# A gated short-convolution layer on one core: SyncE and VectorE held to the plan's order in the first stage, high part's products first

## The chip, the core and the metric

The kernel runs on one core of one Trainium2 chip. The metric is the device time of one execution in microseconds (us). Five engines work side by side: TensorE (PE in the profile, with its weight loads as PEld), VectorE (DVE), ScalarE (ACT), GpSimd (POOL) and SyncE (SP), which here does nothing but issue DMA transfers. Each engine takes its instructions strictly in the order in which they stand on it, and waits at an instruction whose semaphores are not yet there; what stands behind waits too.

## The reference

One layer of a decoder trunk (T = 256 tokens, D = 2048, E = 4096), all in float32:

```
h    = rmsnorm(x, norm_g)                                # (256, 2048)
mod  = silu(c) @ ada_w + ada_b                           # (6144): shift, scale, gate
h    = h * (1 + scale) + shift
b, cg, v, g = split(h @ sc_w_in, 4)                      # four parts of (256, 4096)
u    = causal_conv(cg * v, sc_conv_w)                    # width 3, each channel by itself
y    = (b * u * silu(g)) @ sc_w_out                      # (256, 2048)
out  = rmsnorm(x + gate * y, final_g)
```

## The kernel before

**Precision.** Every float32 product is made of three products of a reduced float32 form (fp32r). A weight is split into a high part (a cast on ScalarE, `split_hi`, L356) and a low part (weight minus high part on VectorE, `split_lo`, L361); the tokens are split the same way (`hh_` and `hl_`, both in the tile hT). A product is high x high, high x low tokens, low x high tokens: three matmuls, all from line L496.

**Stages.** The first stage (up to about 378 us) makes the first 16 of the 32 column tiles of all four parts; the second stage (tile mm_b) makes the other 16; the third multiplies with w_out and ends the layer. The change is in the first stage alone.

**Why the first stage is cut into passes.** The tokens can be multiplied only when shift and scale are known, and for these 32 MB of ada_w have to be read. So the 16 blocks of 128 token features (k = 0 to 15) become ready two at a time. A group of two blocks takes eight *adaLN pieces*: each is two transfers of 256 KB on SyncE (L464, tile at, four buffers) and two weighted sums on VectorE (L476 and L478, tile gv). After the eighth, `ada_done` transposes the sums on TensorE (L486, tp_g), adds them up on VectorE (L487, gs), adds the biases (L326, mod), and makes the block's high part on ScalarE (L330) and its low part on VectorE (L334 scales, L337 subtracts).

A *pass* (`part`) is for one chunk of 512 columns (ch) of one of the four parts (q), over the blocks k0 to k1 that are ready; there are 16 pairs of ch and q. The weights come from w_in by SyncE in slots (L540, tile raw_s): a full slot holds four blocks of 128 x 512 (1 MB), a half slot two (512 KB). A block costs 12 matmuls (`chunk_products`: four column tiles m, three products each). The pass's result in PSUM (mm_s) is kept: the first pass of a pair is copied by ScalarE (L518, tile acc, named by ch and q: acc20 is chunk 2, part 0). A later pass either starts with that sum in PSUM (a *seed*, a copy by ScalarE, L530, before the pass, and L518 behind it) or is added by VectorE (L520).

**What sets the order.** `plan()` walks through the stage with costs from constants (LOAD and ALOAD for transfers, PRODUCTS for a block's matmuls, and so on) and returns a list of steps, passes and adaLN pieces mixed: the earlier tokens are ready, the more blocks the later passes take. The code is written out in this order. But the scheduler of the tile framework then orders each engine's instructions by its own estimates; pieces have a lower priority (`later(GIVE)`), the end of a group a higher one (`later(-LEAD)`). Only the part before the first pass is fixed (`in_order`), and a few casts and low parts are held behind named instructions (`behind`): the casts of passes 2 to 9 behind the copy of the pass three before them, the low parts of passes 4 and 5 behind an adaLN sum.

In this document pass n is the n-th pass in the plan. Up to pass 19 the passes have the same blocks in both plans. Passes 1 to 13 take blocks 0 and 1 (24 matmuls each), 14 to 16 take blocks 0 to 3 (48), 17 to 19 blocks 2 and 3 (24).

The order of matmuls in a pass before: for each block, each m, the three products in turn, so that the low part is needed by the third matmul. Passes 2 and 3 alone do all products of the high part first.

Of the kernel before, what the change touches and what calls it, by code (L numbers as in the profile page):

```python
# [17 lines left out]
KT = D // P  # L18
# [15 lines left out]

LOAD = 0.19
ALOAD = 1.55
PRODUCTS = 0.343
VBLOCK = 0.143  # L40
VPIECE = 1.5
# [1 line left out]
SBLOCK = 0.119  # L43
SCOPY = 1.03
SSEED = 2.05
WLAG = 6.0
ALAG = 9.0
WAHEAD = 14.0
AAHEAD = 6.0
# [2 lines left out]
def plan():  # L52
# [4 lines left out]
    steps, ready = [], [0.0] * ADA[0]  # L57
    done = {}
    pieces = [(sum(ADA[:g]), nk, i) for g, nk in enumerate(ADA) if g for i in range(4 * nk)]
    load, pe, dve, act = 0.0, 4.0, 0.0, 0.0  # L60
    burst = SLOT // P

    def ada():
# [54 lines left out]
def short_conv_layer(ctx: ExitStack, tc: tile.TileContext, x, c, norm_g, ada_w, ada_b, w_in, conv_w, w_out, final_g, out):  # L118
    nc = tc.nc
# [43 lines left out]
    after = mybir.DependencyInfo(mybir.DependencyClass.NoSync, mybir.DependencyReason.DATA)  # L163

    @contextmanager
    def in_order():

        traced = nc.cur_bb.bb.instructions
        n = len(traced)
        yield  # L170
        last = {}
        for ins in list(traced[n:]):
            if ins.engine in last:
                tc.add_manual_dep(ins, last[ins.engine], after, reason="in order")
            last[ins.engine] = ins.name
        ended.update(last)

    @contextmanager
    def behind(last):
# [17 lines left out]
        col = QUARTERS[0] * E  # L197
        nc.sync.dma_start(raw[:, k * CT * P : (k + 1) * CT * P], w_in[0, k * P : (k + 1) * P, col : col + CT * P])

    ended = {}  # L200
    pinned = ctx.enter_context(ExitStack())
    pinned.enter_context(in_order())

# [247 lines left out]
    acc = {}  # L451
    sums = {}

    def ada_piece(k0, nk, piece):
        w = nk * P
        kk = ASLOT // (2 * w)
        if piece == 0:
            sums[k0] = adap.tile([P, 2, 2 * P], F32, tag="gv", name="gv")
        gv = sums[k0][:, :, 0:w]
        j = piece * kk  # L460
        at = adap.tile([P, ASLOT], F32, tag="at", name="at", bufs=4)
        at4 = at.rearrange("p (k s f) -> p k s f", k=kk, s=2)
        for s in range(2):
            nc.sync.dma_start(at4[:, :, s, :], adas[:, j : j + kk, s, k0 * P : k0 * P + w])  # L464
        with later(GIVE):
            ada_sums(j, kk, at4, gv)
        if j + kk == KT:
            with later(-LEAD):
                ada_done(k0, nk, gv)

    def ada_sums(j, kk, at4, gv):
        for i in range(kk):
            c_k = silu_c[:, j + i : j + i + 1]
            if j + i == 0:
                with behind(ended):
                    nc.vector.tensor_scalar_mul(gv, at4[:, i], c_k)  # L476
            else:
                nc.vector.scalar_tensor_tensor(out=gv, in0=at4[:, i], scalar=c_k, in1=gv, op0=ALU.mult, op1=ALU.add)  # L478
        added.append({ins.engine: ins.name for ins in nc.cur_bb.bb.instructions[-1:]})

    def ada_done(k0, nk, gv):

# [29 lines left out]
    kept, added = [], []  # L512

    def keep(ch, q, k0, bank, seed=False):
        if k0 == 0 or seed:
# [6 lines left out]
    def part(ch, q, k0, k1, seed):  # L522
# [13 lines left out]
        for s0 in range(k0, k1, step):  # L536
            sk = min(step, k1 - s0)
            n = sk * CT * P
            raw, hi, lo = places(n)
            nc.sync.dma_start(  # L540
                raw[:, :n].rearrange("p (k f) -> p k f", k=sk),
                w_in[0, s0 * P : (s0 + sk) * P, col : col + CT * P].rearrange("(k p) f -> p k f", p=P),
            )
            at = len(acc) if k0 == 0 else KT
            with behind(ended if at < 3 else kept[at - 3] if at < 9 else {}):
                split_hi(raw, n, hi)
            with behind(ended if at < 3 else added[at - 3] if at < 5 else {}):
                split_lo(raw, n, hi, lo=lo)
            for parts in ((0, 1), (2,)) if 0 < len(acc) < 3 else ((0, 1, 2),):
                for i in range(sk):  # L550
                    chunk_products(bank, hi, lo, i * CT * P, s0 + i, k0, k1, seed, parts=parts)
        if len(acc) == 1:
# [18 lines left out]
            split_y(ys[-1], vq)  # L571

    LATER = (10, 14)
    whole = [0] * NCH
    for kind, *step in plan():
        if kind == "ada":
            ada_piece(*step)
        else:
# [366 lines left out]
```

## Time and profile before

| | |
|---|---|
| time, median of 3 runs | 903.59 us (902.85 to 903.79) |
| the profiled execution | 903.37 us, of which the span of the trace is 901.6 us |
| TensorE busy | 887.4 us, 98% of the span |
| VectorE, ScalarE, GpSimd busy | 75%, 54%, 9% |
| granted TensorE clock | 1.00 in each stretch from 25 to 727 us |
| moved by DMA | 235.01 MB, mean 261 GB/s |

How to read the rows. A row of the timeline has start, length (both in us), engine, line, operation, output tile <- input tiles, shapes and count; in brackets, how long the engine had been idle before it and what ended that. Rows of successive equal instructions are merged. A matmul's length is longer than the distance to the next one, since matmuls overlap; the distance of starts is what it costs. The same holds in small for VectorE and ScalarE.

### The profile page before, as it was taken

To read this page: it belongs to the slowest core of one execution; us is meant where nothing else is said; L and a number is where in the kernel's file an instruction comes from. 1 tells how busy PE (TensorE), PEld (TensorE's weight loads), DVE (VectorE), ACT (ScalarE), POOL (GpSimd) and SP (SyncE) were. 2 spreads that over 40 slices of the span, in tenths; PEclk is the share of its full clock that TensorE was granted. 3 is DMA by queue.
4 is the path that set the end of the run, shared out by engine and by line. 5 is a ranking of instruction groups with operands and counts; after the bars stand their busy time and mean duration, and the time that the engine had idled before them with its cause. 6 is when DMAs were issued, how large, how long until landed. Compare 5 with 4: busy or idle time off the path is not lost.

```text
span 901.6 us, 16416 instructions
## 1 busy us (share of the span) xinstructions
PE 887.4 (98%) x6997; PEld 850.6 (94%) x6997; DVE 675.3 (75%) x665; ACT 484.9 (54%) x429; POOL 84.8 (9%) x96
## 2 busy tenths in 40 slices
PE   7999999999999999999999999999999999999996
PEld 4899999999999999999999999999999988888885
DVE  5889989888888867765775678565555568879886
ACT  6768866665548856644443434444434445554543
POOL 0000000000000042024224302420000000000000
PEclk9999999999999999999999999999999999999998
DMA  9999999999998588687978898866666476673662
GB/s 307 365 369 368 368 315 348 356 369 352 351 326 289 165 277 250 192 257 229 295 227 247 256 289 269 240 198 197 201 193 188 141 284 222 199 275 123 203 234 94
DMA packets 159610, 235.01 MB, mean 261 GB/s; under 512 B 6900, under 2 KB 105284, under 8 KB 159152
## 3 DMA queue, kind: packets, MB, share of 16 engines
q1 hardware_dynamic: 156368, 226.52, 76.7%
q0 software_dynamic: 3040, 7.39, 2.8%
q8 instruction: 55, 0.90, 0.4%
q14 instruction: 19, 0.16, 0.1%
q10 hardware_dynamic: 128, 0.04, 0.0%
HBM read 224.49 MB, written 2.10 MB: 251 GB/s over the span
## 4 chain that ended last, share of the span: by engine, by line
PE 95%; DMA 3%; SPq 0%; ACT 0%; DVE 0%; issue 0%; ACTq 0%; DVEq 0%
PE mm_b L496 39%; PE mm_s L496 37%; PE mm_w L738 7%; PE mm_o L738 7%; PE mm L738 4%; DMA at<-in_ada_w_dram 2%; DMA x<-in_x_dram 1%; PE tp_g L486 0%; DVE lo L361 0%; SPq L464 0%; ACT hi L356 0%; ACT acc L518 0%; SPq L540 0%; SPq L218 0%; ACT big L852 0%
## 5 line engine op out<-in xcount | busy, mean ns | idle before, releaser
L496 PE MATMUL mm_s<-hT,hi 128*128 128x256 f32 x2048 | 348.4, 277 | 1.1 <-ACT hT L330 1.1
L496 PE MATMUL mm_b<-hT,hi 128*128 128x256 f32 x2048 | 348.2, 276 | 0.0
L496 PEld LDWEIGHTS mm_s<-hT,hi 128*128 128x128 f32 x2048 | 307.2, 188 | 1.3 <-ACT hT L330 1.3
L496 PEld LDWEIGHTS mm_b<-hT,hi 128*128 128x128 f32 x2048 | 308.2, 188 | 0.0
L496 PE MATMUL mm_b<-hT,lo 128*128 128x256 f32 x1024 | 282.8, 276 | 0.0
L496 PE MATMUL mm_s<-hT,lo 128*128 128x256 f32 x1024 | 280.2, 277 | 0.8 <-DVE lo L361 0.8
L356 ACT CAST hi<-raw 128x2048 fp32r<-128x2048 f32 (+1 forms) x66 | 123.7, 1875 | 193.5 <-PE mm_b L496 156.7
L361 DVE TENSOR_TENSOR lo<-raw,hi 128x2048 fp32r<-128x2048 f32 (+1 forms) x66 | 150.4, 2280 | 99.9 <-ACT hi L356 99.3
L496 PEld LDWEIGHTS mm_b<-hT,lo 128*128 128x128 f32 x1024 | 192.2, 188 | 0.0
L496 PEld LDWEIGHTS mm_s<-hT,lo 128*128 128x128 f32 x1024 | 190.7, 188 | 1.2 <-DVE lo L361 1.2
L361 DVE TENSOR_TENSOR lo<-raw_s,hi 128x2048 fp32r<-128x2048 f32 (+1 forms) x80 | 149.5, 1877 | 35.1 <-ACT hi L356 34.6
L356 ACT CAST hi<-raw_s 128x2048 fp32r<-128x2048 f32 (+1 forms) x80 | 124.2, 1558 | 58.2 <-PE mm_s L496 47.2
L478 DVE SCALAR_TENSOR_TENSOR gv<-at,silu_c,gv 128x512 f32<-128x512 f32 x105 | 78.5, 748 | 7.6 <-DMA at<-in_ada_w_dram 5.9
L518 ACT COPY acc<-mm_s 128x1024 f32<-128x1024 f32 x54 | 54.7, 1013 | 39.4 <-PE mm_s L496 39.2
L361 DVE TENSOR_TENSOR lo<-raw_o,hi 128x2048 fp32r<-128x2048 f32 x22 | 50.4, 2290 | 23.4 <-ACT hi L356 23.4
L356 ACT CAST hi<-raw_o 128x2048 fp32r<-128x2048 f32 x22 | 42.0, 1908 | 46.4 <-PE mm_w L738 12.6
L738 PE MATMUL mm_w<-hi,y 128*128 128x512 f32 x184 | 58.8, 389 | 0.0
L634 POOL TENSOR_TENSOR gacc<-gacc,z 128x512 f32<-128x512 f32 x28 | 44.7, 1597 | 116.2 <-DMA z<-gacc 116.2
L738 PE MATMUL mm_o<-hi,y 128*128 128x512 f32 x176 | 55.3, 389 | 0.0
L628 DVE SCALAR_TENSOR_TENSOR gacc<-at_g,silu_c,gacc 128x512 f32<-128x512 f32 x60 | 45.8, 764 | 8.2 <-DMA at_g<-in_ada_w_dram 7.2
L632 POOL DMA_DIRECT2D z<-gacc x28 | 15.6, 556 | 330.5 <-DVE acc L569 283.9
L738 PEld LDWEIGHTS mm_w<-hi,y 128*128 128x128 f32 x184 | 34.5, 188 | 7.2
(154 smaller groups left out, 689.4 us busy)
## 6 DMA issues: line engine op xcount, KB each, us to landing
raw<-in_sc_w_in_dram SPq DMA_DIRECT2D x64, 1024.0 KB, 5.8
raw_s<-in_sc_w_in_dram SPq DMA_DIRECT2D x47, 1024.0 KB, 8.3
raw_o<-in_sc_w_out_dram SPq DMA_DIRECT2D x32, 1024.0 KB, 5.3
at<-in_ada_w_dram SPq DMA_DIRECT2D x126, 256.0 KB, 7.9
raw_s<-in_sc_w_in_dram SPq DMA_DIRECT2D x33, 512.0 KB, 7.2
at_g<-in_ada_w_dram SPq DMA_DIRECT2D x32, 512.0 KB, 8.1
x<-in_x_dram SPq DMA_DIRECT2D x4, 512.0 KB, 6.3
big<-in_x_dram SPq DMA_DIRECT2D x2, 1024.0 KB, 8.2
```

Source lines behind the costliest of these rows:

```text
L356: nc.scalar.copy(hi[:, :n], raw[:, :n])
L361: last_low[0] = nc.vector.tensor_tensor(out=lo[:, :n], in0=raw[:, :n], in1=hi[:, :n].bitcast(F32), op=ALU.subtract)
L478: nc.vector.scalar_tensor_tensor(out=gv, in0=at4[:, i], scalar=c_k, in1=gv, op0=ALU.mult, op1=ALU.add)
L496: mm = last_mm[0] = nc.tensor.matmul(dst, w, h[k], start=begins and left, stop=ends, skip_group_check=True)
L518: nc.scalar.copy(acc[ch, q], bank)
L628: nc.vector.scalar_tensor_tensor(out=ga, in0=at3[:, i, :], scalar=s, in1=ga, op0=ALU.mult, op1=ALU.add)
L632: nc.gpsimd.dma_start(turned[0 : P - away], ga[away:P])
L634: nc.gpsimd.tensor_tensor(out=ga, in0=ga, in1=turned, op=ALU.add)
L738: nc.tensor.matmul(dst, y[a], b, start=opens and i == 0, stop=ends and i == 2, skip_group_check=True)
```

## The change

It changes four things in the first stage.

1. Figures of the plan: a block's load 0.18 instead of 0.19 us, an adaLN piece's 1.45 instead of 1.55, WLAG 4 instead of 6, the start 3 instead of 4. The plan has 51 passes instead of 56. From pass 20 on they take more blocks each (pass 20: blocks 2 to 5 instead of 2 and 3), the last adaLN piece stands after pass 34 instead of 39, and from pass 5 on there is one piece after each pass up to pass 10.
2. From the second step of the plan until the fourteenth pass comes up (`PLANNED`: 13 pairs have been begun), SyncE and VectorE are held to the order in which the plan's steps are written. The end of an adaLN group (`ada_done`) is left out of this (`loose`).
3. Casts are held behind the copy of the pass three before them up to pass 16 instead of 9; low parts are no longer held behind adaLN sums.
4. In every pass the products of the high part come first, for all blocks of a slot, and then those of the low part.

```diff
-LOAD = 0.19
-ALOAD = 1.55
+LOAD = 0.18
+ALOAD = 1.45
...
-WLAG = 6.0
+WLAG = 4.0
...
-    load, pe, dve, act = 0.0, 4.0, 0.0, 0.0
+    load, pe, dve, act = 0.0, 3.0, 0.0, 0.0
...
-    def in_order():
+    def in_order(engines=None):
...
         for ins in list(traced[n:]):
+            if engines is not None and (ins.engine not in engines or ins.name in loose):
+                continue
             if ins.engine in last:
                 tc.add_manual_dep(ins, last[ins.engine], after, reason="in order")
             last[ins.engine] = ins.name
-        ended.update(last)
+        if engines is None:
+            ended.update(last)
...
+            traced = nc.cur_bb.bb.instructions
+            n = len(traced)
             with later(-LEAD):
                 ada_done(k0, nk, gv)
+            loose.update(ins.name for ins in traced[n:])
...
-            with behind(ended if at < 3 else kept[at - 3] if at < 9 else {}):
+            with behind(ended if at < 3 else kept[at - 3] if at < KT else {}):
                 split_hi(raw, n, hi)
-            with behind(ended if at < 3 else added[at - 3] if at < 5 else {}):
+            with behind(ended if at < 3 else {}):
                 split_lo(raw, n, hi, lo=lo)
-            for parts in ((0, 1), (2,)) if 0 < len(acc) < 3 else ((0, 1, 2),):
+            for parts in ((0, 1), (2,)):
                 for i in range(sk):
                     chunk_products(bank, hi, lo, i * CT * P, s0 + i, k0, k1, seed, parts=parts)
...
+    PLANNED = 13
     whole = [0] * NCH
-    for kind, *step in plan():
+    planned = ExitStack()
+    for n, (kind, *step) in enumerate(plan()):
+        if n == 1:
+            planned.enter_context(in_order((mybir.EngineType.SP, nc.vector.engine)))
+        elif kind == "mm" and len(acc) == PLANNED:
+            planned.close()
```

What this moves is seen in the order of the instructions on each engine. First SyncE, from the load of pass 4 on. An at row with x2 is one adaLN piece, a raw_s row of 128x2x512 the half slot of one pass, 128x4x512 the full slot of pass 14. Before:

```order
L540 DMA raw_s<-in_sc_w_in_dram 128x2x512
L464 DMA at<-in_ada_w_dram 128x2x256 x2
L540 DMA raw_s<-in_sc_w_in_dram 128x2x512
L464 DMA at<-in_ada_w_dram 128x2x256 x4
L540 DMA raw_s<-in_sc_w_in_dram 128x2x512 x4
L464 DMA at<-in_ada_w_dram 128x2x256 x4
L540 DMA raw_s<-in_sc_w_in_dram 128x2x512 x2
L464 DMA at<-in_ada_w_dram 128x2x256 x4
L540 DMA raw_s<-in_sc_w_in_dram 128x2x512 x2
L464 DMA at<-in_ada_w_dram 128x2x256 x2
L540 DMA raw_s<-in_sc_w_in_dram 128x4x512
```

And now, up to pass 9:

```order
L545 DMA raw_s<-in_sc_w_in_dram 128x2x512
L467 DMA at<-in_ada_w_dram 128x2x256 x2
L545 DMA raw_s<-in_sc_w_in_dram 128x2x512
L467 DMA at<-in_ada_w_dram 128x2x256 x2
L545 DMA raw_s<-in_sc_w_in_dram 128x2x512
L467 DMA at<-in_ada_w_dram 128x2x256 x2
L545 DMA raw_s<-in_sc_w_in_dram 128x2x512
L467 DMA at<-in_ada_w_dram 128x2x256 x2
L545 DMA raw_s<-in_sc_w_in_dram 128x2x512
L467 DMA at<-in_ada_w_dram 128x2x256 x2
L545 DMA raw_s<-in_sc_w_in_dram 128x2x512
```

Loads and pieces now alternate one by one, and between the loads of passes 5 and 14 stand eight pieces instead of seven.

Second, ScalarE around the cast of pass 14 (the first of 128x2048). acc22, acc23, acc20 and acc31 are the copies of passes 10, 11, 12 and 13; the number behind a name counts buffers. Before:

```order
L518 COPY acc22_625<-mm_s_594 128x1024
L356 CAST hi_666<-raw_s_665 128x1024
L518 COPY acc23_657<-mm_s_629 128x1024
L356 CAST hi_754<-raw_s_753 128x2048
L330 ACTIVATE hT_173<-xs0_175,mod_179 128x256 x2
L518 COPY acc20_695<-mm_s_664 128x1024
L518 COPY acc31_744<-mm_s_716 128x1024
```

And now:

```order
L523 COPY acc22_630<-mm_s_599 128x1024
L359 CAST hi_685<-raw_s_684 128x1024
L333 ACTIVATE hT_173<-xs0_175,mod_179 128x256 x2
L359 CAST hi_685<-raw_s_684 128x1024
L523 COPY acc23_681<-mm_s_653 128x1024
L523 COPY acc20_714<-mm_s_683 128x1024
L359 CAST hi_759<-raw_s_758 128x2048
L523 COPY acc31_750<-mm_s_722 128x1024
```

The cast of pass 14 now stands behind the copy of pass 12; before, it stood in front of it.

Third, VectorE around the second token group (blocks 4 and 5): acc_342 is the sum of pass 18, gs and mod end the group, xs_176 and hT are its low tokens. Before:

```order
L520 TENSOR_TENSOR acc_342<-mm_s,acc_342 128x1024
L361 TENSOR_TENSOR lo<-raw_s,hi 128x1024
L487 TENSOR_REDUCE gs<-tp_g 128x4
L326 TENSOR_TENSOR mod<-gs,vec 128x2x2
L478 SCALAR_TENSOR_TENSOR gv<-at,silu_c,gv 128x512 x2
L361 TENSOR_TENSOR lo<-raw_s,hi 128x2048
L334 TENSOR_SCALAR xs_176<-xs_176,mod 128x256 x2
L337 TENSOR_TENSOR hT<-xs_176,hT 128x256
```

And now:

```order
L492 TENSOR_REDUCE gs<-tp_g 128x4
L329 TENSOR_TENSOR mod<-gs,vec 128x2x2
L525 TENSOR_TENSOR acc_342<-mm_s,acc_342 128x1024
L484 SCALAR_TENSOR_TENSOR gv<-at,silu_c,gv 128x512
L364 TENSOR_TENSOR lo<-raw_s,hi 128x2048
L337 TENSOR_SCALAR xs_176<-xs_176,mod 128x256
L484 SCALAR_TENSOR_TENSOR gv<-at,silu_c,gv 128x512
L337 TENSOR_SCALAR xs_176<-xs_176,mod 128x256
L340 TENSOR_TENSOR hT<-xs_176,hT 128x256
```

The group's end has moved in front of the sum of pass 18; its low tokens still stand behind that sum, one update and one low part, with an update between them. On TensorE they are now first used in pass 20, where before it was pass 22.

More of the change, by code (lines that the diff above doesn't have):

```diff
@@ L198, in first_load @@
         nc.sync.dma_start(raw[:, k * CT * P : (k + 1) * CT * P], w_in[0, k * P : (k + 1) * P, col : col + CT * P])
-    ended = {}
+    ended, loose = {}, set()
     pinned = ctx.enter_context(ExitStack())
@@ L478, in ada_sums @@
                 nc.vector.scalar_tensor_tensor(out=gv, in0=at4[:, i], scalar=c_k, in1=gv, op0=ALU.mult, op1=ALU.add)
-        added.append({ins.engine: ins.name for ins in nc.cur_bb.bb.instructions[-1:]})
     def ada_done(k0, nk, gv):
@@ L511, in short_conv_layer @@
     last_mm = [None]
-    kept, added = [], []
+    kept = []
     def keep(ch, q, k0, bank, seed=False):
```

## The prediction

> **What bounds the kernel now.** The page comes first: its engine row, and the row that sums the chain that ended last.
>
> ```profile
> PE 887.4 (98%) x6997; PEld 850.6 (94%) x6997; DVE 675.3 (75%) x665; ACT 484.9 (54%) x429; POOL 84.8 (9%) x96
> PE 95%; DMA 3%; SPq 0%; ACT 0%; DVE 0%; issue 0%; ACTq 0%; DVEq 0%
> ```
>
> TensorE is 98% busy and makes up 95% of the chain. The change removes no matmul, so it can win only time in which TensorE waits. The windows view, by stage (columns: length, then busy time of PE, PEld, DVE, ACT, POOL, granted clock, DMA share, GB/s), and the view of waits from 24 to 385 us say where:
>
> ```profile
> 25.00:34.00 9.00, 8.72 (x75) 8.53 (x75) 6.90 (x10) 7.83 (x12) 1.53 (x2) 1.00 1.06 354
> 34.00:60.00 26.00, 25.47 (x222) 25.27 (x223) 22.75 (x27) 19.41 (x20) 0.00 (x0) 1.00 1.06 371
> 60.00:92.00 32.00, 32.00 (x283) 31.97 (x282) 30.44 (x38) 24.52 (x25) 0.00 (x0) 1.00 1.07 368
> 92.00:130.00 38.00, 38.00 (x337) 38.00 (x336) 33.68 (x39) 28.35 (x25) 0.00 (x0) 1.00 1.01 341
> 130.00:240.00 110.00, 110.00 (x971) 110.00 (x970) 97.26 (x110) 66.09 (x56) 0.00 (x0) 1.00 1.04 355
> 240.00:378.00 138.00, 138.00 (x1220) 138.00 (x1219) 108.11 (x112) 93.15 (x91) 17.48 (x21) 1.00 0.80 257
> 378.00:727.00 349.00, 349.00 (x3080) 348.94 (x3079) 219.66 (x193) 146.48 (x114) 65.13 (x67) 1.00 0.74 228
> ...
> PE mm_s L496 <- ACT hT L330: 1.1, 1, 1.1
> PE mm_s L496 <- DVE lo L361: 0.8, 2, 0.5
> ```
>
> From 60 to 727 us TensorE has no idle time. The 1.1 us lie before the first pass, where both kernels are alike. There remain two waits for VectorE's low parts, both between 25 and 60 us, where the transfers are saturated too (share 1.06). TensorE's timeline prices them:
>
> ```profile
> 30.61 1.98 PE L496 MATMUL mm_s<-hT,hi 128*128 128x256 f32 x16
> 32.42 1.07 PE L496 MATMUL mm_s<-hT,lo 128*128 128x256 f32 x8
> 33.33 0.39 PE L496 MATMUL mm_s<-hT,hi 128*128 128x256 f32 x2
> 33.98 0.39 PE L496 MATMUL mm_s<-hT,lo 128*128 128x256 f32 x1 [0.27 <-DVE lo L361]
> 34.21 0.39 PE L496 MATMUL mm_s<-hT,hi 128*128 128x256 f32 x2
> ...
> 36.60 0.39 PE L496 MATMUL mm_s<-hT,hi 128*128 128x256 f32 x2
> ...
> 39.33 0.39 PE L496 MATMUL mm_s<-hT,hi 128*128 128x256 f32 x2
> 40.24 0.39 PE L496 MATMUL mm_s<-hT,lo 128*128 128x256 f32 x1 [0.53 <-DVE lo L361]
> 40.47 0.39 PE L496 MATMUL mm_s<-hT,hi 128*128 128x256 f32 x2
> ```
>
> A matmul costs 0.113 us from start to start (32.42 - 30.61 = 1.81 for 16), so a short pass of 24 takes 2.72. The third matmul of pass 4 starts at 33.98 where 33.33 + 0.23 was possible: 0.42 lost, and 0.12 more before the next one (0.23 instead of 0.11). In pass 6, 0.68 and 0.12. Together 1.34 us: that is all the change can win.
>
> **Product order.** Pass 3, at 30.61, already has the new order (16 products of the high part, then 8 of the low) and runs at the same 0.113: the order itself costs nothing. It moves due times. The low part of a half slot is first needed 1.81 us into its pass instead of 0.23. But where a pass reaches into new tokens, these are needed sooner: 16 products of two old blocks go first, not 24, so 0.9 us earlier.
>
> **The two waits go.** VectorE's and ScalarE's timelines:
>
> ```profile
> 32.04 0.75 DVE L478 SCALAR_TENSOR_TENSOR gv<-at,silu_c,gv 128x512 f32<-128x512 f32 x1 [1.44 <-DMA at<-in_ada_w_dram]
> 32.71 1.22 DVE L361 TENSOR_TENSOR lo<-raw_s,hi 128x1024 fp32r<-128x1024 f32 x1
> ...
> 33.48 1.05 ACT L356 CAST hi<-raw_s 128x1024 fp32r<-128x1024 f32 x1 [1.03 <-DMA raw_s<-in_sc_w_in_dram]
> 36.80 1.02 ACT L518 COPY acc<-mm_s 128x1024 f32<-128x1024 f32 x1 [1.37 <-PE mm_s L496]
> 37.88 1.05 ACT L356 CAST hi<-raw_s 128x1024 fp32r<-128x1024 f32 x1
> ```
>
> Pass 4's low part stood behind a sum update that waited 1.44 us for its transfer. In the plan's order it stands in front, and it is needed only at 33.33 + 1.81 = 35.14; even at the old 33.93 it would be 1.2 us early. Pass 6's load had two adaLN pieces between it and pass 5's and now has one; half a MB less is 1.4 us at 371 GB/s; its low part is needed 1.6 us later in the pass, and the pass begins 0.54 earlier: 2.5 us of cover against 0.68 lost. Term: **-1.34**.
>
> **What VectorE's fixed order can hold up.** A sum update that waits for its piece now holds the low parts behind it, and through them TensorE. From pass 5 to 10 the plan puts one piece after each pass: 0.5 MB each, so 2.83 us of transfers per pass at 371 GB/s against 2.72 us of matmuls, a loss of 0.11 per pass. Pass 5's load is there at 33.48 (its cast had waited for it) and cast by 34.53, for a pass that begins at 33.33 + 2.72 = 36.05: a lead of 1.5 us. Five such passes take 0.6 of it, which is also the price if that lead weren't there. Taken as 0. On SyncE loads now stand behind a piece that waits for one of its four buffers:
>
> ```profile
> at<-in_ada_w_dram SPq DMA_DIRECT2D x126, 256.0 KB, 7.9
> ```
>
> A piece's half lands 7.9 us after its issue though it moves in 0.7 (256 KB at 371 GB/s). Most of that is queue, so an issue a few us late leaves no gap: 0 again.
>
> **Pass 14 is late by its cast (L356).** It loads a whole slot of 1 MB. In the new ScalarE order its cast stands behind the copy of pass 12, which is ready only when pass 13 begins.
>
> ```profile
> 43.06 1.02 ACT L518 COPY acc<-mm_s 128x1024 f32<-128x1024 f32 x1 [0.97 <-PE mm_s L496]
> 43.97 1.05 ACT L356 CAST hi<-raw_s 128x1024 fp32r<-128x1024 f32 x1
> 57.96 1.92 ACT L356 CAST hi<-raw_s 128x2048 fp32r<-128x2048 f32 x1 [0.29 <-DMA raw_s<-in_sc_w_in_dram]
> ...
> 56.74 0.44 PE tp_g L486 x4
> ```
>
> The copy starts 0.20 us into the next pass (36.80 after 36.60), the cast 0.91 later (43.97 - 43.06) and takes 1.92; TensorE starts 0.05 after (33.98 against 32.71 + 1.22). Ready at 3.08 us; pass 13 lasts 2.72: 0.36 late, and with the 0.12 of a restart **+0.48**. The load must be there too. Pass 13 begins at 33.33 + 9 x 2.72 + 0.44 (four transposes) = 58.25, so the cast begins at 59.36. Between pass 5's load and this one's end lie 8 pieces, 8 half slots and 1 MB, 9.44 MB: 25.4 us at 371 GB/s, so 58.9, just in time. Under 364 GB/s the transfer sets the wait, and pass 15 (two pieces and 1 MB, 2.1 MB against 5.44 us of matmuls) adds to it.
>
> By the Trainium skill ("DMA: Bandwidth & Descriptors", Specifications) a core gets about 358 GB/s from HBM. By that rate the load would land at 59.8, passes 14 and 15 would wait 0.9 and 0.4 us, and the sum below would be +1.4. The trace disagrees, with 371 and 368 GB/s in these two windows.
>
> **Pass 20 now needs fresh tokens.** It reaches to block 6 instead of 4, so its 18th matmul wants the low half of block 4. VectorE makes that behind the sum of pass 18 (ready only at pass 18's end), a sum update and a low part of 2048. The same steps in the trace:
>
> ```profile
> 84.37 0.39 PE L496 MATMUL mm_s<-hT,hi 128*128 128x256 f32 x2
> ...
> 84.57 1.23 DVE L520 TENSOR_TENSOR acc<-mm_s,acc 128x1024 f32<-128x1024 f32 x1 [0.86 <-PE mm_s L496]
> 85.71 1.22 DVE L361 TENSOR_TENSOR lo<-raw_s,hi 128x1024 fp32r<-128x1024 f32 x1
> ...
> 89.10 2.29 DVE L361 TENSOR_TENSOR lo<-raw_s,hi 128x2048 fp32r<-128x2048 f32 x1
> 91.30 0.73 DVE L334 TENSOR_SCALAR xs<-xs,mod 128x256 f32<-128x256 f32 x2
> 91.95 0.42 DVE L337 TENSOR_TENSOR hT<-xs,hT 128x256 fp32r<-128x256 f32 x1
> 92.29 0.74 DVE L478 SCALAR_TENSOR_TENSOR gv<-at,silu_c,gv 128x512 f32<-128x512 f32 x1
> 92.95 0.42 DVE L337 TENSOR_TENSOR hT<-xs,hT 128x256 fp32r<-128x256 f32 x1
> ...
> 96.50 3.90 DVE L478 SCALAR_TENSOR_TENSOR gv<-at,silu_c,gv 128x512 f32<-128x512 f32 x5
> ```
>
> Counted from the start of pass 19, by starts: the sum begins at 0.20 (84.57 - 84.37); then sum 1.14, update 0.66, low part 2.20, scale 0.33, update 0.66, scale 0.33, subtraction 0.42, and 0.05 to TensorE: 5.99 us. TensorE is there after 24 + 17 matmuls, 4.65. It waits 1.34, with the restart **+1.46**. Updates that follow their own sum take 0.79 ((3.90 - 0.75) / 4), which could add 0.26. Before, no pass came near: block 4 was first used in pass 22. Of the 1.46, 0.9 comes from the product order.
>
> **The rest.** Twelve copies and one cast fewer on ScalarE, one sum more on VectorE: hidden while the loads are ahead. Counting bytes in SyncE's new order at 370 GB/s and 0.34 us per product block, pass 22's load lands 5 us before its pass begins. Taken as 0; at most a restart or two, 0.12 each.
>
> **Sum.** -1.34 + 0.48 + 1.46 = **+0.60 us**, bounds +0.36 (no restarts) to +0.86 (the slow updates). The profiled execution took 903.37, so 903.97; it lies inside the runs shown, 0.22 under their median of 903.59. On the median: **904.2 us**, 903.95 to 904.45.
>
> **The rivals.** *All waits go*: neither new wait appears, because transposes and casts come earlier than my count. Then -1.34: 902.25. For it: nothing waits between 60 and 378 us today. Against: both new waits follow from rows that stand in a fixed order.
>
> *The load of pass 14 comes late*: the transfers run at the 355 GB/s of the window from 130 to 240. It lands at 60.0, passes 14 and 15 wait 1.17 and 0.45 instead of 0.48: +1.74, so 905.3. For it: the pipe is full (share 1.06), and an execution need not repeat 371. Against: 371 and 368 where it counts. The skill's section above is on this rival's side.
>
> *The transfers become the bound (slower)*: the pieces now ahead of passes 14 and 15 cost more than counted. At 341 GB/s (window 92 to 130) the load lands at 61.1 and its cast ends at 63.0; pass 14 waits 2.2, pass 15 0.7: +3.0, so 906.6. It decides from 354 GB/s down, the rate of the first window, where the sum passes +1.8. For it: the pipe, full from the start, carries more pieces early than before. Against: the same two windows.
>
> *It doesn't do what it says*: 903.6; the rows of the changed order speak against it.
>
> **How the numbers follow.** Forecast 0.68, all waits go 0.10, late load 0.10, transfers bind 0.10, no effect 0.02. About 0.2% (1.8 us) is what a measurement of this kernel can tell from no change. Even the win of 1.34 is under it, so faster gets 0.03, out of the first rival; slower has the transfers' 0.10 and half of the late load's 0.10, which ends just under the line; the same has 0.82. The range runs from 902.2, the full win, to 906.0, short of the transfers' 906.6.
>
> **What would show it.** Right: the view of waits after has no VectorE wait near 34 and 40 us, one for ScalarE's cast near 61 of about 0.4 us, and one for VectorE's token block (line 340) near 90 of about 1.3 us; then full windows. Wrong: waits for weights between 41 and 58 us, a cast at pass 14 released by its transfer, waits after 95 us, or no wait near 90 us.

## The result, and the profile after

The changed kernel takes 904.64 us (median; 904.03 to 908.1 in 22 runs), the kernel before in runs on the same chip 903.24 us (902.72 to 904.06 in 22). The ratio is 1.0018, with a 95% interval of 1.0013 to 1.0024: the interval lies above 1, so the changed kernel is slower, by 1.4 us on the medians. The forecast was +0.60. The profiled execution took 904.62 us, with a span of 902.8, so 1.2 longer than the one before.

The page of after: the engine row, and the row that sums the chain.

```profile
PE 887.5 (98%) x6997; PEld 851.1 (94%) x6997; DVE 676.1 (75%) x665; ACT 472.0 (52%) x416; POOL 89.9 (10%) x96
PE 94%; DMA 3%; DVE 1%; ACT 1%; issue 1%; SPq 0%; ACTq 0%; DVEq 0%
```

Windows of after (length, then PE, PEld, DVE, ACT, POOL, granted clock, DMA share, GB/s), and its view of waits from 24 to 385 us:

```profile
25.00:34.00 9.00, 9.00 (x79) 9.00 (x80) 7.37 (x10) 8.06 (x12) 1.52 (x2) 1.00 1.07 366
34.00:60.00 26.00, 26.00 (x229) 26.00 (x228) 23.49 (x32) 19.11 (x22) 0.00 (x0) 1.00 1.07 367
60.00:92.00 32.00, 30.75 (x264) 30.35 (x263) 29.03 (x34) 24.18 (x22) 0.00 (x0) 1.00 1.07 369
92.00:130.00 38.00, 38.00 (x337) 38.00 (x337) 34.88 (x39) 22.28 (x20) 0.00 (x0) 1.00 1.03 345
```

```profile
PE mm_s L501 <- DVE hT L340: 1.2, 1, 1.2
PE mm_s L501 <- ACT hT L333: 1.1, 1, 1.1
```

The idle time has moved from the first two windows to the third, as forecast: none before 60 us, 1.25 between 60 and 92, none after. (The 1.1 us lie ahead of the first pass in both kernels.) The two new places are the forecast ones. Pass 14 first, on ScalarE and on TensorE:

```profile
58.55 1.02 ACT L523 COPY acc<-mm_s 128x1024 f32<-128x1024 f32 x1 [1.29 <-PE mm_s L501]
59.47 1.91 ACT L359 CAST hi<-raw_s 128x2048 fp32r<-128x2048 f32 x1
```

```profile
49.53 1.98 PE L501 MATMUL mm_s<-hT,hi 128*128 128x256 f32 x16
51.35 1.08 PE L501 MATMUL mm_s<-hT,lo 128*128 128x256 f32 x8
...
55.52 2.04 PE L501 MATMUL mm_s<-hT,hi 128*128 128x256 f32 x16
57.41 1.10 PE L501 MATMUL mm_s<-hT,lo 128*128 128x256 f32 x8
58.35 2.04 PE L501 MATMUL mm_s<-hT,hi 128*128 128x256 f32 x16
60.24 1.10 PE L501 MATMUL mm_s<-hT,lo 128*128 128x256 f32 x8
61.43 4.04 PE L501 MATMUL mm_s<-hT,hi 128*128 128x256 f32 x32
...
71.08 2.04 PE L501 MATMUL mm_s<-hT,lo 128*128 128x256 f32 x16
72.96 2.22 PE L501 MATMUL mm_s<-hT,hi 128*128 128x256 f32 x18
```

Pass 13 starts at 58.35, the copy 0.20 later, the cast 0.92 after that with no bracket (its data were there), and pass 14 starts at 61.43, that is 3.08 after pass 13: the forecast figure. The view of waits has no row for it, because the row at 60.24 ends at 61.34 and leaves only 0.09 us of idle time; the wait is read from the cast's end (59.47 + 1.91 = 61.38), 0.05 before TensorE starts. In these rows stands also what was not forecast. From 49.53 to 51.35, 16 matmuls cost 1.82 us, 0.114 each; from 55.52 to 57.41, and again from 58.35 to 60.24 and from 71.08 to 72.96, 16 cost 1.89, 1.89 and 1.88: 0.118 each, at a granted clock of 1.00.

Pass 20 next, VectorE and TensorE:

```profile
84.54 1.23 DVE L525 TENSOR_TENSOR acc<-mm_s,acc 128x1024 f32<-128x1024 f32 x1 [0.17 <-PE mm_s L501]
85.68 0.74 DVE L484 SCALAR_TENSOR_TENSOR gv<-at,silu_c,gv 128x512 f32<-128x512 f32 x1
86.34 2.29 DVE L364 TENSOR_TENSOR lo<-raw_s,hi 128x2048 fp32r<-128x2048 f32 x1
88.54 0.41 DVE L337 TENSOR_SCALAR xs<-xs,mod 128x256 f32<-128x256 f32 x1
88.86 0.75 DVE L484 SCALAR_TENSOR_TENSOR gv<-at,silu_c,gv 128x512 f32<-128x512 f32 x1
89.52 0.41 DVE L337 TENSOR_SCALAR xs<-xs,mod 128x256 f32<-128x256 f32 x1
89.85 0.42 DVE L340 TENSOR_TENSOR hT<-xs,hT 128x256 fp32r<-128x256 f32 x1
```

```profile
84.34 1.99 PE L501 MATMUL mm_s<-hT,hi 128*128 128x256 f32 x16
86.17 1.07 PE L501 MATMUL mm_s<-hT,lo 128*128 128x256 f32 x8
87.07 2.09 PE L501 MATMUL mm_s<-hT,hi 128*128 128x256 f32 x17
90.32 1.88 PE L501 MATMUL mm_s<-hT,hi 128*128 128x256 f32 x14 [1.16 <-DVE hT L340]
```

From the start of pass 19 (84.34) to the first product with the low half of block 4 (90.32) it is 5.98 us; the forecast was 5.99.

**Where the 1.23 us went.** The stage's matmuls run from 25.01 to 378.29 before and from 24.90 to 379.41 after, 353.28 and 354.51 us; the second stage is as long in both (348.16). In the distances of successive matmul starts the difference splits into three parts. *Waits* with their restarts (distances over 125 ns, without the first pass and the restarts behind transposes): 1.46 before (0.43 + 0.11 and 0.69 + 0.12 in passes 4 and 6, a restart of 0.11 at 73.8), 1.80 after (0.26 + 0.11 in pass 14, 1.32 + 0.11 in pass 20), **+0.34**. *Slower spacing* (distances of 116 to 125 ns, what they have over 113.3): 60 matmuls and 0.35 us before, 284 and 1.31 after, **+0.97**. Transposes and rounding: -0.08. The sum is +1.23.

### The profile page after: what moved, and what is told of

Read it like the earlier page. It is cut to its first block, busy times and chain, and to the rows that moved or that the text cites. A ratio compares the mean times of both kernels' runs of the same rounds, so it can differ in the third digit from the quotient of the medians.

```text
span 902.8 us, 16395 instructions
## 1 busy us (share of the span) xinstructions
PE 887.5 (98%) x6997; PEld 851.1 (94%) x6997; DVE 676.1 (75%) x665; ACT 472.0 (52%) x416; POOL 89.9 (10%) x96
## 4 chain that ended last, share of the span: by engine, by line
PE 94%; DMA 3%; DVE 1%; ACT 1%; issue 1%; SPq 0%; ACTq 0%; DVEq 0%
PE mm_b L501 39%; PE mm_s L501 38%; PE mm_w L749 7%; PE mm_o L749 6%; PE mm L749 4%; DMA at<-in_ada_w_dram 1%; DMA raw_o<-in_sc_w_out_dram 1%; DMA x<-in_x_dram 1%; ACT hi L359 0%; DMA raw_s<-in_sc_w_in_dram 0%; PE tp_g L491 0%; DVE lo L364 0%; DVE lo L780 0%; ACT hi L777 0%; DVE sums_o L772 0%
## 5 line engine op out<-in xcount | busy, mean ns | idle before, releaser
L501 PE MATMUL mm_s<-hT,hi 128*128 128x256 f32 x2048 | 247.5, 277 | 2.4 <-DVE hT L340 1.2
L501 PEld LDWEIGHTS mm_s<-hT,hi 128*128 128x128 f32 x2048 | 239.3, 188 | 3.0 <-DVE hT L340 1.4
L364 DVE TENSOR_TENSOR lo<-raw,hi 128x2048 fp32r<-128x2048 f32 (+1 forms) x66 | 152.3, 2309 | 93.4 <-ACT hi L359 92.8
L501 PE MATMUL mm_s<-hT,lo 128*128 128x256 f32 x1024 | 130.3, 277 | 0.0
L501 PEld LDWEIGHTS mm_s<-hT,lo 128*128 128x128 f32 x1024 | 122.7, 188 | 0.0
L523 ACT COPY acc<-mm_s 128x1024 f32<-128x1024 f32 x48 | 48.7, 1014 | 43.1 <-PE mm_s L501 42.9
L645 POOL TENSOR_TENSOR gacc<-gacc,z 128x512 f32<-128x512 f32 x28 | 48.6, 1734 | 112.6 <-DMA z<-gacc 112.6
```

The lines of the kernel that those rows point to most:

```text
L364: last_low[0] = nc.vector.tensor_tensor(out=lo[:, :n], in0=raw[:, :n], in1=hi[:, :n].bitcast(F32), op=ALU.subtract)
L501: mm = last_mm[0] = nc.tensor.matmul(dst, w, h[k], start=begins and left, stop=ends, skip_group_check=True)
L523: nc.scalar.copy(acc[ch, q], bank)
L645: nc.gpsimd.tensor_tensor(out=ga, in0=ga, in1=turned, op=ALU.add)
```

## The experiments

The question was where the slower spacing comes from, and whether the waits have the causes that the prediction gave them. The kernels combine three things: the plan's figures, the fixed order of SyncE and VectorE, and the product order (*by m*: the three products of each column tile in turn; *by piece*: 16 or 32 of the high part, then 8 or 16 of the low; *by block*: 8, then 4). Waits and excess are counted as above, in one profiled execution each; in brackets the longest stretch of slower spacing, in matmuls less than 1 us apart. Each trace has all 3072 matmuls of the stage.

| kernel | plan | fixed | products | median us | ratio to before, 95% | waits us | excess us (longest) | stage 1 us |
|---|---|---|---|---|---|---|---|---|
| before | old | no | by m | 903.24 | | 1.46 | 0.35 (8) | 353.28 |
| b_new_order | old | no | by piece | 902.72 | 0.9992, 0.9984 to 1.0001 | 0.08 | 0.72 (79) | 352.24 |
| h_short | old | no | by piece to pass 13 | 902.63 | 0.9992, 0.9983 to 1.0001 | 0.51 | 0.37 (9) | 352.32 |
| n_blocks | old | no | by block | 902.47 | 0.9990, 0.9982 to 0.9999 | 0.01 | 0.32 (13) | 351.77 |
| e_old_plan | old | yes | by piece | 904.28 | 1.0013, 1.0004 to 1.0022 | 1.79 | 1.01 (91) | 354.24 |
| f_plan_only | new | no | by m | 904.48 | 1.0013, 1.0004 to 1.0022 | 2.28 | 0.51 (9) | 354.18 |
| g_no_order | new | no | by piece | 908.35 | 1.0045, 1.0029 to 1.0062 | 5.84 | 1.31 (146) | 358.53 |
| a_old_order | new | yes | by m | 907.5 | 1.0046, 1.0033 to 1.0059 | 3.86 | 0.44 (9) | 355.70 |
| d_short_only | new | yes | by piece to pass 13 | 906.53 | 1.0032, 1.0020 to 1.0045 | 3.79 | 0.40 (8) | 355.58 |
| t_after_blocks | new | yes | by block | 904.7 | 1.0013, 1.0004 to 1.0022 | 2.37 | 0.47 (19) | 354.23 |
| after | new | yes | by piece | 904.64 | 1.0018, 1.0013 to 1.0024 | 1.80 | 1.31 (167) | 354.51 |
| c_cast9 | new | yes | by piece | 904.4 | 1.0010, 1.0001 to 1.0018 | 1.90 | 1.01 (96) | 354.29 |
| p_tokens | new | yes | by piece | 903.6 | 1.0010, 1.0001 to 1.0018 | 0.48 | 1.20 (95) | 353.06 |
| s_copy12 | new | yes | by piece | 908.75 | 1.0067, 1.0050 to 1.0084 | 5.56 | 0.93 (63) | 357.88 |

The medians move with the length of the stage, but only to within about 1 us, and in a_old_order to within 1.8 (median 4.2 over the kernel before in the same runs, stage 2.4 over). The third stage, which no edit touches, lasts 167.3 to 168.1 us in these traces, with waits near 752, 785 and 842 us that differ from one to the next. And in the four kernels that wait longest (g_no_order, s_copy12, a_old_order, d_short_only) 12 of 25 runs have a mean granted clock of 0.995 or 0.996, where of all other runs with a clock on record only one, of the kernel before, is under 0.997. Their medians may hold lost clock beside the waits, which of their traces only that of g_no_order shows. So smaller differences are read from the stage's own rows, not from the medians.

### The product order undone, and done alone

a_old_order, on the changed kernel:

```diff
-            for parts in ((0, 1), (2,)):
+            for parts in ((0, 1), (2,)) if 0 < len(acc) < 3 else ((0, 1, 2),):
```

> The changed kernel with the old product order from pass 4 on (each output block takes its three products at once); new plan figures and fixed SyncE and VectorE order stay. In the traces the changed kernel's first stage is 1.23 us longer than the one before: its waits are 0.45 us more (1.80 against 1.35), and some 290 of its matmuls follow at 117 to 119 ns instead of 113 (1.33 us of excess; before 0.36 in 62 matmuls). Theory (the new product order keeps the slower spacing going): the excess falls back to about 0.4, the wait near 90 us shrinks from 1.4 to about 0.5, the one near 61 us stays; the kernel ends about 1.9 us under the changed one, 0.7 under the kernel before. Rival (the slower spacing comes with the fixed order or with the new plan's transfers): the excess stays at about 1.3; only the 0.9 of the wait goes, so 0.3 over the kernel before.

b_new_order is the reverse edit on the kernel before.

> The kernel before with the new product order in all passes, and nothing else. Theory (the order keeps the slower spacing going): the waits near 34 and 40 us go (the low part is needed 1.6 us later), -1.35, and the excess of the spacing rises from 0.36 to about 1.3, +1.0: 0.2 to 0.5 us under the kernel before. Rival (the spacing comes with the fixed order or the new plan): the excess stays at about 0.4, so 1.2 to 1.4 us under the kernel before.

The spacing went the way that the theory said: by m it is back at 0.44 (longest stretch 9), by piece it rises to 0.72 (79), though 1.3 was expected. The waits of a_old_order did not, and its time is far over both forecasts. Without the product order the changed kernel waits 3.86 us, at places where neither kernel did: passes 7 and 10 (0.53 and 0.53, with 0.11 each for the restart), the cast of pass 14 (0.36), and 1.99 for pass 14's low part. The view of waits, then the chain at pass 10, on ScalarE, VectorE and TensorE:

```profile
PE mm_s L501 <- DVE lo L364: 2.6, 3, 1.8
```

```profile
47.55 1.02 ACT L523 COPY acc<-mm_s 128x1024 f32<-128x1024 f32 x1 [1.15 <-PE mm_s L501]
48.46 1.05 ACT L359 CAST hi<-raw_s 128x1024 fp32r<-128x1024 f32 x1
```

```profile
49.55 1.23 DVE L364 TENSOR_TENSOR lo<-raw_s,hi 128x1024 fp32r<-128x1024 f32 x1 [0.83 <-ACT hi L359]
```

```profile
50.83 0.39 PE L501 MATMUL mm_s<-hT,lo 128*128 128x256 f32 x1 [0.37 <-DVE lo L364]
```

The copy of pass 8 can begin only 0.20 us into pass 9 (47.35), the cast 0.91 later, the low part 1.09 after that, and TensorE starts 1.28 after this: 3.48 us for a pass of 2.72 that wants its low part 0.23 in. It is 0.53 late. By piece the low part is wanted 1.81 in, and the same chain has 1.05 us to spare. So the product order is what makes the rest of the change bearable: with it the same plan and the same fixed order take 2.9 us less on the medians (904.64 against 907.5), 1.2 of it in the stage's rows (354.51 against 355.70). Done alone it takes away every wait of the stage (0.08 left): of the two waits that the change removes, neither needs the fixed order or the new figures. It gave back 0.37 in spacing, and the interval of the ratio still reaches 1.0001.

### The plan's figures and the fixed order, one without the other

e_old_plan, on the changed kernel; f_plan_only is the reverse edit on the kernel before:

```diff
-LOAD = 0.18
-ALOAD = 1.45
+LOAD = 0.19
+ALOAD = 1.55
...
-WLAG = 4.0
+WLAG = 6.0
...
-    load, pe, dve, act = 0.0, 3.0, 0.0, 0.0
+    load, pe, dve, act = 0.0, 4.0, 0.0, 0.0
```

> The changed kernel with the old four figures of the plan; fixed order and new product order stay. The old plan puts two adaLN pieces ahead of pass 6 and reaches block 4 first in pass 22, not 20. Theory: the wait near 90 us (1.4) goes with the plan's figures; with a fixed order a sum update ahead of a low part costs little because the low part is needed 1.8 us into a pass; the excess of the spacing stays near 1.3. So about 1.4 us under the changed kernel, within 0.3 of the kernel before. Rival (the spacing comes with the new plan): its excess falls to about 0.4 too, about 2.4 under the changed kernel, 1.1 under the kernel before.

> The kernel before with the new four figures of the plan alone; the old product order, VectorE and SyncE free to be ordered as before. Theory: two waits for low parts of about 0.5 each stay or move among passes 4 to 8, block 4 is first used in pass 20 and waits about 0.5 there (0.9 less than with the new product order); spacing excess about 0.4: 0.3 to 0.8 us over the kernel before. Rival (the spacing comes with the new plan's transfers): 1.0 more, 1.3 to 1.8 over.

With the old plan the wait near 90 us is gone, as expected, but another of 1.21 + 0.11 stands at 63.26: pass 14 wants a token block whose subtraction stands behind the 2.29 us low part of the same pass. With the new figures alone, pass 6 still waits (0.75 + 0.11 at 39.04; SyncE, free to be ordered, still has two pieces ahead of its load), pass 4 hardly (0.08 + 0.11), and pass 20 waits 0.94 + 0.11 for its low part at 87.39. The excess was 1.01 by piece and 0.51 by m: the plan is not what sets the spacing. On the medians e_old_plan is 1.0 and f_plan_only 1.2 us over the kernel before, both more than was expected.

g_no_order leaves out the line that enters `in_order` for SyncE and VectorE.

> The changed kernel without the fixed order of SyncE and VectorE; new plan figures and new product order stay. Theory A (the prediction's working: the wait near 90 us stands in VectorE's fixed order, behind the sum of pass 18, an update and a low part): without the order the scheduler may put the token block ahead, the wait shrinks to 0.5 or less; the wait near 61 us (0.37) stays, since ScalarE's copies and casts stay as they are. About 1.0 us under the changed kernel. Theory B (the wait comes from the plan's reach and the product order, whoever orders VectorE): with the new figures alone and the old product order pass 20 already waited 0.94 for its first low part; then a wait of 0.9 to 1.9 stays near 88 us, and the time is within 0.5 of the changed kernel. The slower spacing stays at 1.0 or more in both.

Theory A fell, since the wait near 90 us grew; theory B, which had the time within 0.5 of the changed kernel, was too low: 908.35. Its waits, and VectorE's rows near pass 20:

```profile
PE mm_s L501 <- DVE hT L340: 2.4, 1, 2.4
PE mm_s L501 <- ACT hi L359: 1.2, 1, 1.2
```

```profile
83.81 1.22 DVE L525 TENSOR_TENSOR acc<-mm_s,acc 128x1024 f32<-128x1024 f32 x1 [2.19 <-PE mm_s L501]
85.03 2.29 DVE L364 TENSOR_TENSOR lo<-raw_s,hi 128x2048 fp32r<-128x2048 f32 x1
...
88.23 2.28 DVE L364 TENSOR_TENSOR lo<-raw_s,hi 128x2048 fp32r<-128x2048 f32 x1
...
91.95 2.28 DVE L364 TENSOR_TENSOR lo<-raw_s,hi 128x2048 fp32r<-128x2048 f32 x1
...
96.13 0.75 DVE L340 TENSOR_TENSOR hT<-xs,hT 128x256 fp32r<-128x256 f32 x2
```

Left free, the scheduler puts three low parts of 2.28 us ahead of the token blocks, which come at 96.13 instead of 89.85. Of its 5.84 us, 1.6 are no wait: from 98.0 to 101.5 us, 1.4 us after the longest of these waits ended and 4 us after it began, 17 matmuls stand about 0.21 us apart. The granted clock is 0.50 from 98.0 to 101.3, which brings the whole window to 0.96:

```profile
92.00:130.00 38.00, 35.62 (x297) 0.96 0.99 326
```

The fixed order ends with pass 13, yet what it leaves behind decides the rows near 90 us: with the new plan and the product order it is worth 3.7 us on the medians and 4.0 in the stage, the 1.6 of slowed matmuls included. With the old plan it costs 1.6 on the medians and 2.0 in the stage (e_old_plan against b_new_order).

### The two new waits, taken apart

c_cast9 holds casts behind the copy of the pass three before them up to pass 9 only (`at < 9` for `at < KT`).

> The changed kernel with one limit put back: casts are held behind the copy of two passes before up to pass 9 only, not up to pass 20. Theory (the prediction's step on pass 14: its cast is late by the copy of pass 12): the wait near 61 us (0.37) goes, and nothing else moves: 0.2 to 0.4 us under the changed kernel, with the wait near 90 us at 1.4 or up to 0.4 more. Rival (pass 14 is late by its transfer): the wait stays, the same time.

The wait stayed (0.36, and long enough here for a row in the view of waits), but that does not speak for the rival: every engine's instructions stand in the same order as in the changed kernel, so the scheduler puts the cast behind the copy of pass 12 with or without the hold. The run is therefore a second trace of the changed kernel's order. Both waits come back to within 0.1 us (1.32 again in pass 20); the excess is 1.01 instead of 1.31, its long stretch beginning at 61.7 instead of 52.1 us and ending at 73.2 in both.

```profile
PE mm_s L501 <- ACT hi L359: 0.2, 1, 0.2
```

s_copy12 lets VectorE copy the sum of pass 12 (`nc.vector.tensor_copy` where `len(acc) == 12`).

> The changed kernel with the sum of pass 12 copied out by VectorE instead of ScalarE. Holding casts behind copies up to pass 9 only left every engine's order and the wait near 61 us as they were (0.36, before that 0.26). Theory (pass 14's cast is late by the copy of pass 12 in front of it on ScalarE, wherever that order comes from): the cast starts about 1 us sooner, and the wait near 61 us goes. Rival (the cast is late by its transfer): it stays at 0.3 or more. For the whole kernel no forecast: the free order after pass 14 comes out differently too (the wait near 90 us may move).

ScalarE's timeline:

```profile
58.69 1.90 ACT L359 CAST hi<-raw_s 128x2048 fp32r<-128x2048 f32 x1 [1.60 <-DMA raw_s<-in_sc_w_in_dram]
```

Without the copy in front, the cast starts when its transfer lands, at 58.69, and would be done at 60.6, before TensorE asked for it in the changed kernel (61.06). So the copy, which held the changed kernel's cast until 59.47, 0.78 us later than the transfer, is what made pass 14 late. That the wait would vanish is worked out and not shown: VectorE's copy made pass 13's low part 1.92 late here, so pass 14 began later in any case.

p_tokens adds one order: the low part of pass 20 behind the low tokens of blocks 4 and 5.

```diff
             loose.update(ins.name for ins in traced[n:])
+            fresh.append({ins.engine: ins.name for ins in traced[n:]})
...
-            with behind(ended if at < 3 else {}):
+            with behind(ended if at < 3 else fresh[1] if len(kept) == 19 else {}):
```

> The changed kernel with one order added on VectorE: the low part of pass 20 stands behind the token blocks 4 and 5, not ahead of them. Theory (the wait near 90 us is the low half of block 4 standing behind the 2.2 us low part): the first subtraction is done by about 88.1 us instead of 90.3, and pass 20 asks for it at 88.9: the wait of 1.4 goes; the low part is done at about 90.7 and asked for at about 90.6, so 0 to 0.3 comes back. 1.1 to 1.4 us under the changed kernel, the wait near 61 us stays. Rival (block 4 is late through ScalarE's activation or the transposes): the wait stays above 1 us, the same time.

VectorE's timeline:

```profile
86.37 0.41 DVE L337 TENSOR_SCALAR xs<-xs,mod 128x256 f32<-128x256 f32 x1
...
87.68 0.75 DVE L340 TENSOR_TENSOR hT<-xs,hT 128x256 fp32r<-128x256 f32 x2
88.35 2.29 DVE L364 TENSOR_TENSOR lo<-raw_s,hi 128x2048 fp32r<-128x2048 f32 x1
```

The wait near 90 us is gone and nothing took its place: the stage is 1.45 us shorter and the median 1.0, where 1.1 to 1.4 was expected. So the low part in front of the token block was its cause, as the prediction had it.

### The spacing, and the cover

d_short_only (on the changed kernel) and h_short (on the kernel before) have the order by piece only up to pass 13 (`0 < len(acc) < 13`).

> The changed kernel with the new product order only up to pass 13 (the passes of one half slot); from pass 14 on each output block takes its three products at once. Theory (the new order keeps the slower spacing going and asks for new tokens 0.9 us sooner): no stretch of slower spacing longer than ten matmuls after 62 us, the excess falls from 1.33 to about 0.8; the wait near 90 us falls by 0.9 to about 0.5. But pass 14 then wants its low part 0.23 us into the pass and not after 32 products (3.6 us): with the old order everywhere it waited 2.0 us there, so it does here. Sum: -0.5 -0.9 +2.1 = +0.7 over the changed kernel. Rival (pass 14's low part was late in that run only because the passes before it had waited): no wait there, 1.4 under the changed kernel.

> The kernel before with the new product order up to pass 13 only; nothing else. With the new order in all passes it had no wait left in the first stage (1.35 before) and 0.72 of slower spacing (before 0.35), and took 0.54 us less. Theory (the spacing after 62 us is the order's): no wait near 34 and 40 us, the excess back at about 0.35: 0.4 under the kernel with the new order everywhere, 0.9 to 1.3 under the kernel before. Rival (the long stretch from 63 to 73 us came from something else than the order): excess 0.7 as there, 0.5 under the kernel before. If pass 14 needs the cover of the new order, a wait near 62 us takes up to 2 us back.

Both have the excess of the order by m (0.40 and 0.37, no stretch over 9). h_short has no named wait left; restarts of 0.09 to 0.11 us, at 66.6 and 285 us above all, make up its 0.51. d_short_only waits 0.73 for a low part near 89 us, and 2.3 us for pass 14's low part, which the order by piece covers with 32 products (3.6 us):

```profile
63.83 0.39 PE L501 MATMUL mm_s<-hT,lo 128*128 128x256 f32 x1 [2.17 <-DVE lo L364]
```

The forecasts of the times were off in both: d_short_only is 1.9 us over the changed kernel on the medians (1.1 in the stage, expected 0.7), h_short 0.7 under the kernel before (1.0 in the stage, expected 0.9 to 1.3).

The order by block stands between the two. t_after_blocks has, on the changed kernel, only the two loops exchanged; n_blocks writes the same two loops into the kernel before, in place of its order by m:

```diff
-            for parts in ((0, 1), (2,)):
-                for i in range(sk):
+            for i in range(sk):
+                for parts in ((0, 1), (2,)):
```

> The kernel before with the high part's products first in each token block (8, then 4 of the low part), in all passes, not in each piece. Theory (long runs of the same kind of product keep the slower spacing going; runs of three do not): between the two, an excess of 0.35 to 0.7. The low part of a half slot is needed 0.9 us into its pass, not 0.23 and not 1.81; before, the two waits were 0.43 and 0.69, so the first goes and the second may leave 0 to 0.1. In all 0.5 to 1.2 us under the kernel before. Rival (only the order of three products block by block recovers): the excess at 0.7 or more, as with the new order.

> The changed kernel with the high part's products first in each token block (8, then 4), not in each piece (16 or 32, then 8 or 16). Theory of the spacing (long runs of one kind keep it slow): no stretch over 20 matmuls, excess 0.3 to 0.5 where the changed kernel had 1.3 and 1.0 in two looks. Theory of the cover (with VectorE's fixed order the low parts come 0.5 us too late for a need 0.23 us into a pass, and 2.0 to 2.3 us too late for pass 14): needed 0.9 us into the pass, no wait near 41 and 50 us, but one of 1.3 to 1.7 near 62 us, beside the 0.36 of the cast; the wait near 90 us falls by up to 0.9 and by what was lost before. In all 0 to 1.5 us under the changed kernel. Rivals: the excess stays at 1.0 or more; no wait near 62 us.

t_after_blocks has an excess of 0.47 (longest stretch 19) where the changed kernel had 1.31 and 1.01, no wait near 41 or 50 us, and 1.30 + 0.11 at 62.06 for pass 14's low part, which now has 0.9 us of cover instead of 3.6. The stage is 0.28 us shorter than the changed kernel's and the median the same (0 to 1.5 under was expected). The cast's wait (0.35 + 0.11) stays, and near 90 us 0.38 + 0.11 is left, for a low part:

```profile
63.47 0.72 PE L501 MATMUL mm_s<-hT,lo 128*128 128x256 f32 x4 [1.14 <-DVE lo L364]
```

n_blocks is the only kernel here whose interval lies wholly below 1, 0.9982 to 0.9999. Its page and its view of waits:

```profile
PE 886.7 (99%) x6997; PEld 850.4 (95%) x6997; DVE 674.8 (75%) x665; ACT 484.5 (54%) x429; POOL 87.9 (10%) x96
```

```profile
PE mm_s L496 <- ACT hT L330: 1.2, 1, 1.2
```

No wait is left between the first pass and the end of the stage, and the spacing is that of the kernel before. That is a gain of about 0.7 us on the medians and 1.5 in the stage, by the order of the products alone, with neither a new plan nor a fixed order.

The spacing shows in one row each. The window from 61.5 to 73 us has no idle time in any of four kernels, and the same clock; the count of matmuls is what differs. Before, by m:

```profile
61.50:73.00 11.50, 11.50 (x104) 1.00 1.07 372
```

After, by piece:

```profile
61.50:73.00 11.50, 11.50 (x98) 1.00 1.07 370
```

b_new_order, by piece:

```profile
61.50:73.00 11.50, 11.50 (x100) 1.00 1.07 374
```

n_blocks, by block:

```profile
61.50:73.00 11.50, 11.50 (x103) 1.00 1.06 373
```

Each count takes in one transpose, and also the matmuls that were still running when the window began: three, but only one in the row of after, where TensorE had just waited. Matmuls that start in the window are 100 before, 96 after, 96 in b_new_order and 99 in n_blocks. Four fewer after than before, in 11.5 us of "full" TensorE, are 0.45 us; the excess of the slower spacing there is 0.42.

## Why the prediction was right or wrong

**Right in the places and sizes of the waits.** *The two waits go*: neither is left, 1.35 gone of the 1.34 forecast. *Pass 14 is late by its cast*: +0.37, forecast 0.48; the cast came exactly at the forecast 3.08 us after pass 13's start, and the wait was 0.11 smaller because pass 13 took 2.83 us at the slower spacing and not 2.72. *Pass 20 needs fresh tokens*: +1.43, forecast 1.46, through the very rows that were counted, and p_tokens removed it by moving one of them. *The rest*: no wait for weights between 41 and 58 us, none after 95, as said; the one restart of 0.11 at 73.8 that the kernel before had is gone.

**Wrong in one step: "the order itself costs nothing".** Between the traces of before and after it cost +0.97 us, more than the whole forecast sum; in the second trace of the same order (c_cast9) it is +0.66, and alone on the kernel before (b_new_order) +0.37. The step took one pass of 24 matmuls (0.113 each) as proof for 3000. The spacing depends on what came before: in all seven kernels that run passes 14 and later by m or by block the excess is 0.32 to 0.51 and no stretch is longer than 19; in all seven that run them by piece it is 0.72 to 1.31, with a stretch of 63 to 167. The plan and the fixed order do not sort them so. One order gave 1.31 and 1.01 in two traces, so the step from 0.51 to 0.72 is a small one; that from 19 to 63 matmuls is not. And long runs of one kind allow the slower spacing, they do not force it: the longest stretches of g_no_order (from 38.7 us) and s_copy12 (from 52.0) lie ahead of pass 14, in passes that d_short_only and h_short also run by piece with no stretch over 9. What the order does to the spacing is shown by undoing it; by what mechanism stays open.

**Right, but not for the whole reason: why the two waits go.** Pass 4 was put down to VectorE's order, pass 6 to the load that comes half a MB sooner and to the later need. Either half does it alone: a_old_order, with the order and the load and without the later need, has no wait in passes 4 to 6, and b_new_order, with the later need alone, has none either. What the prediction counted for pass 14 (as far as the cast) and not for the short passes is the chain of copy, cast and low part, 3.48 us in passes of 2.72: without the later need it puts waits of the same size into passes 7 and 10. The conclusion held because the product order was part of the change.

**The rivals.** *All waits go* did not happen in the changed kernel. *The load of pass 14 comes late* and *the transfers become the bound* needed less than 364 and 354 GB/s; the windows from 25 to 92 us show 366, 367 and 369, and the load landed at 58.69 in s_copy12, where 58.9 was forecast. The Trainium skill's 358 GB/s ("DMA: Bandwidth & Descriptors", Specifications) stays under what these windows moved.

**The time.** Forecast 904.2, measured 904.64, inside the range of 902.2 to 906.0, but above what the sum's own bounds allow (903.95 to 904.45). That it came so near is in part luck: the kernel before ran at 903.24 in these runs, 0.35 under the 903.59 from which the forecast counts. Against the kernel before in the same runs the forecast of +0.60 was 0.8 too small: 0.97 of spacing was not counted, and waits and transposes came to +0.26 and not +0.60. That leaves 0.63 for the stage; the other 0.17 is what the difference of the medians (1.40) has over that of the stage in the two traces (1.23).

## What to carry to other kernels

An order that puts the late operand last buys cover for the engine that makes it, but give it no more than it needs: in the kernel before, 8 and 4 products took away both waits as 16 and 8 did, and kept TensorE's step, while with the fixed order pass 14 needed the longer cover. Read a "full" TensorE by the matmuls that start in a window, not by its busy time: a count that falls by 4% at the same clock is a loss that no view of waits shows. And when several edits go together, do each alone before crediting a gain: the one-line order alone took every wait away and ended 0.5 us under the kernel before (not quite clear of no change), and with the plan and the fixed order that came with it the kernel ended 1.4 us over.

## What the runs showed of the hardware

Matmuls of this one shape follow each other at 113 ns or at about 118 ns at the same granted clock (1.00). Most rows of the slower kind last 279 to 281 ns instead of 276. It begins behind transposes or a wait, when the stream starts again. In passes by m it ends within nine matmuls in every trace here; in long runs of one kind of product it can go on for 167. Two traces of one instruction order began the long stretch at different restarts (52.1 and 61.7 us) and ended it at the same pass boundary (73.2). What ends it was not found: some passes by piece come back to 113 ns within four matmuls and others do not, from the same kind of start.

In g_no_order, 1.4 and 2.7 us between matmul starts at 90.3 and 93.9 us were followed, 4 us after the second one began, by 3.5 us of matmuls at half the rate, with a granted clock of 0.50 from 98.0 to 101.3 us. s_copy12, with 1.5 and 2.0 us at 91.8 and 95.5, did not show it; one trace each leaves open where the point lies.
